# Seven-product projections at the front, and prompt attention A and B two heads at a time in halves of TensorE's array

## The chip, the core and the metric

The kernel runs on one core of a Trainium2 chip. The metric is the device time of one execution in microseconds (us). A core has TensorE (PE; its weight loads are PEld), VectorE (DVE), ScalarE (ACT), GpSimd (POOL) and SyncE (SP, which issues most DMAs), and 16 DMA engines.

## What is computed

One layer of a streaming encoder, on 1024 prompt frames and 8 x 16 sample frames (1152 rows, nine tiles of 128), width 1024:

```python
def project(xn, w_in, b_f, g_qa, g_ka, g_qb, g_kb, g_qm):
    z = xn @ w_in
    qa, ka, va, qb, kb, vb, fl, qm, gates = jnp.split(z, IN_SPLITS, axis=-1)
    qa = rmsnorm(qa.reshape(b, t, H_A, DH_A), g_qa)
...
def gated_merge(o_a, o_b, o_m, gates, w_pa, w_pb, w_pm, w_o):
    g_a, g_b, g_m = jnp.split(jax.nn.sigmoid(gates), N_BRANCH, axis=-1)
    h = g_a * (o_a @ w_pa) + g_b * (o_b @ w_pb) + g_m * (o_m @ w_pm)
    return h @ w_o
...
    xp = xp + gated_merge(o_a, o_b, o_m, gates, w_pa[l], w_pb[l], w_pm[l], w_o[l])
    xp = xp + sq_relu_mlp(xp, g_ffn[l], w_up[l], w_down[l])
```

ka, qb, kb and qm are normalised like qa, and sq_relu_mlp is the square of relu(rmsnorm(x) w_up), times w_down. o_a is attention in a band of nine 64-frame chunks (8 heads of 64, a learned bias by distance), o_b causal attention with summed forget gates added to the scores (8 heads of 64), o_m cross attention into 256 memory tokens (4 heads of 128). Each is computed for the prompt and for the samples, which also read caches. Q and K are normalised per head. K, V, the forget gates and the memory's K and V are outputs too. Everything is float32.

## The kernel before

Most products are made of three matmuls in a fast float32 format (F32R): each operand is split into a high part (ACT copies it to F32R) and a low part (DVE or POOL subtracts), and hi·hi, hi·lo and lo·hi are added in PSUM (`hilo` line 270, `mm3` line 322). Plain float32 matmuls are used for transposes and in the sample attentions.

**Stages.** First the front: x is scaled and split (`x_part`), then `group` (line 387) multiplies, for each of nine row tiles, eight depth tiles of x with a 512-wide block of w_in: V_A, Q_A, K_A, the memory's K and V, and V_B with the eight forget-gate columns (two halves of 260). `head_norm` (line 353) does squares, sums, a power on POOL and two multiplications; `to_T` transposes Q and K and stores them in DRAM.

Then prompt A, sample A, prompt B, sample B, memory for the prompt and the samples: six attentions one after another (`attend`, line 1560). Their engines' orders are written ahead by a planner (`class Plan`, line 50). It runs the attention's tasks against a small cost table, hands each piece to TensorE when its inputs should be ready, and where none is ready takes a *filler* (`fill`, line 133): single depth steps of other products. Fillers are, in this order, `project` (line 624: Q_B, K_B and Q_M, each in two halves 256 wide, with their norms and transposes), `gates` (line 586: 24 feature tiles times three columns of 384 frames, tanh, stored in DRAM) and `merge` (line 723: the products with w_pa, w_pb, w_pm and the gated sum). The order so made is kept on TensorE, DVE, ACT, POOL and SP.

After the last filler come the output projection with w_o and the MLP, which is already done by seven products in place of eight (`Pair`, `DOWN`).

**Prompt A and B** (`prompt_ab`, line 840) run 64 steps: 8 heads times 8 query blocks of 128. For one step: `scores` (line 914) multiplies the block's queries with up to 640 (A) or 1024 (B) keys, in pieces of at most 512, `soften` adds the bias and takes the maximum on DVE, `exp_norm` does the exponential on ACT and the division on POOL or DVE, `transposes` (line 964) turns the probabilities by blocks of 128, `values` (line 1007) multiplies two query blocks at once with V. A head has only 64 dimensions, so the kernel fills the 128 rows twice: Q's high part stands in rows 0 to 63 and its low part in rows 64 to 127 (`qs`), K stands in both halves (`kh`, `kl`), and two matmuls of all rows make the product:

```python
pe.matmul(ps[:, :m], qa, kh[:, ks], start=True, stop=False)
pe.matmul(ps[:, :m], qa, kl[:, ks], start=False, stop=True)
```

V stands likewise in the columns (`vs`: 64 of high part, 64 of low part); the turned probabilities are split into `pth` (ACT) and `ptl` (DVE) on their way out of PSUM, two matmuls a key block, and ACT and DVE add the two halves of the result. PSUM's eight banks are divided z 2 (fillers), tp 3 (transposes), s 2 (scores), pv 1 (values).

The sample attentions place four small float32 matmuls beside each other, in quarters of the array's columns (`tile_position=(0, 32 * pr)`).

Of the kernel before, what the change touches and what calls it, by code (L numbers as in the profile page):

```python
# [49 lines left out]
class Plan:  # L50
# [50 lines left out]
    def bank(self, k):  # L101
        r = self.rel[k]
        return r[len(r) - self.bufs[k]] if len(r) >= self.bufs[k] else 0.0
# [82 lines left out]
def tile_encoder(ctx: ExitStack, tc: tile.TileContext, i, o):  # L186
    nc = tc.nc
    plan = Plan()

    class Engine:  # L190
# [4 lines left out]
        def __getattr__(self, name):  # L195
            f = getattr(self.e, name)

            def call(*a, **k):
                ins = f(*a, **k)  # L199
                if plan.on:  # L200
                    tc.keep_in_program_order(ins)
                return ins
            return call

    class pe:
        @staticmethod
        def matmul(out, lhsT, rhs, **k):
            n = math.prod(rhs.shape[1:])
            plan.now += n * ((2 if "tile_position" in k else 4) if rhs.dtype == F32 else 2 if n < 256 else 1) / 2400 + 0.003
            ins = nc.tensor.matmul(out, lhsT, rhs, **k)  # L210
            if plan.on:
                tc.keep_in_program_order(ins)

        @staticmethod
        def transpose(*a):
            plan.now += math.prod(a[0].shape[1:]) * 2 / 2400
            ins = nc.tensor.transpose(*a)
            if plan.on:
                tc.keep_in_program_order(ins)
# [31 lines left out]
    def banks(**n):  # L251
        with ExitStack() as st:
# [7 lines left out]
    gains = tl(cst, (P, 512), tag="gains")  # L260
    g_of = {"qa": gains[:, 0:64], "qb": gains[:, 64:128], "ka": gains[:, 128:192], "kb": gains[:, 192:256],
            "qm": gains[:, 256:384], "km": gains[:, 384:512]}
# [70 lines left out]
    rm = tl(cst, (P, 2), tag="rm")  # L333
    prj = ExitStack()

    pgs = ExitStack()
    pg = pgs.enter_context(tc.tile_pool(reuse_waits="tile", name="pg", bufs=2, side="right"))
    rb = tl(pg, (P, NT), tag="rb", bufs=1)
    pxs = ExitStack()
    px = pxs.enter_context(tc.tile_pool(reuse_waits="tile", name="px", bufs=2, side="right"))  # L340
    pj = prj.enter_context(tc.tile_pool(reuse_waits="tile", name="pj", bufs=2))
    wp = prj.enter_context(weights(3, 14, "wp"))
    prj.enter_context(banks(z=4, tp=3))
# [4 lines left out]
    for _ in range(18):  # L348
        pe.matmul(ps[:, 0, :], idle, idle, start=True, stop=True)
# [3 lines left out]
    def head_norm(z, sc, gain, dh):  # L353

        nh = HB // dh
        zc = tl(pj, (P, HB), tag="zc")
        act.activation(zc, z, AF.Copy, scale=sc)
        sq = tl(pj, (P, HB), tag="sq", bufs=1)
        act.activation(sq, zc, AF.Square)
        ss = tl(pj, (P, 8), tag="hss")  # L360
        vec.tensor_reduce(ss[:, :nh], sq.rearrange("p (h d) -> p h d", h=nh), AX.X, ALU.add)
        r = tl(pj, (P, 8), tag="hr")
        rstd(ss[:, :nh], r[:, :nh], dh)
        zn = tl(pj, (P, HB), tag="zn", bufs=5)
        v3 = lambda t: t.rearrange("p (h d) -> p h d", h=nh)
        vec.tensor_tensor(v3(zn), v3(zc), r[:, :nh, None].to_broadcast((P, nh, dh)), ALU.mult)
        gps.tensor_tensor(v3(zn), v3(zn), gain[:, None, :].to_broadcast((P, nh, dh)), ALU.mult)
        return zn

    def to_T(zn, dst, t):  # L370
# [4 lines left out]
        act.activation(zt, ps, AF.Copy)  # L375
        act.dma_start(dst.rearrange("(k p) t -> p k t", p=P)[:, :, t * P:(t + 1) * P], zt)


    later = []

    def flush(keep=0):
        while len(later) > keep:
            f = later.pop(0)
            if f:
                f()

    def group(ws, n, handle, pair=None, tiles=TT):
        nb = 2 if n > 512 else 1
        m = n // nb
        for t in range(tiles):  # L390
            zs = []
            for b in range(nb):
                ps = tl(psum["z"], (P, 512), tag="z")
                lhs = cols(xp, t) if pair is None else (lambda k: tuple(s[:, k, t * P:(t + 1) * P] for s in pair))
                mm3(ps[:, :m], lhs, lambda k: tuple(w[:, b * m:(b + 1) * m] for w in ws[k]), KD)
                zs.append(ps[:, :m])
            flush(2)
            later.append(handle(t, *zs))

    def w_rows(src, col, n):  # L400
        return [weight(wp, src[k * P:(k + 1) * P, col:col + n], n) for k in range(KD)]

    def q_tile(b, dh):
        def handle(t, z):
            zn = head_norm(z, rs[:, t:t + 1], g_of["q" + b], dh)
            return lambda: to_T(zn, qT[b], t)
        return handle

    def k_tile(b):
        def handle(t, z):  # L410
            zn = head_norm(z, rs[:, t:t + 1], g_of["k" + b], 64)
            sp.dma_start(o["k" + b][t * P:(t + 1) * P, :], zn)
            return lambda: to_T(zn, kT[b], t)
        return handle

    def v_a(t, z):
        zn = tl(pj, (P, HB), tag="zv")
        act.activation(zn, z, AF.Copy, scale=rs[:, t:t + 1])
        act.dma_start(o["va"][t * P:(t + 1) * P, :], zn)

    def v_b(t, z0, z1):
        zn = tl(pj, (P, HB), tag="zv")
        act.activation(zn[:, 0:260], z0, AF.Copy, scale=rs[:, t:t + 1])
        act.activation(zn[:, 260:512], z1[:, 0:252], AF.Copy, scale=rs[:, t:t + 1])
        act.dma_start(o["vb"][t * P:(t + 1) * P, :], zn)
        vec.scalar_tensor_tensor(lf[:, t, :], z1[:, 252:260], rs[:, t:t + 1], bf, ALU.mult, ALU.add)

    def mem_k(t, z):
        zn = head_norm(z, rm[:, t:t + 1], g_of["km"], 128)
        sp.dma_start(o["mk"][t * P:(t + 1) * P, :], zn)  # L430
        return lambda: to_T(zn, mkT, t)

    def mem_v(t, z):
        zn = tl(pj, (P, HB), tag="zv")
        act.activation(zn, z, AF.Copy, scale=rm[:, t:t + 1])
        act.dma_start(o["mv"][t * P:(t + 1) * P, :], zn)
# [60 lines left out]
    def x_part(c, kh, ks=range(4)):  # L497
        xr = tl(px, (P, 4, CH), tag="xr")
        ks = list(ks)
        k0, k1 = ks[0], ks[-1] + 1  # L500
        src = i["xT"].rearrange("(k p) t -> p k t", p=P)
        sp.dma_start(xr[:, k0:k1, :], src[:, kh * 4 + k0:kh * 4 + k1, c * CH:(c + 1) * CH])
        for k in ks:
            hilo_scaled(xr[:, k, :], xp[0][c][kh][:, k, :], xp[1][c][kh * 4 + k], gcol[:, 0, kh * 4 + k:kh * 4 + k + 1])

    def x_rows(ts):
        for t in ts:
            xt = tl(px, (P, D), tag="xt")
            sp.dma_start(xt, i["x"][t * P:(t + 1) * P, :])
            sum_sq(px, xt, ss[:, t:t + 1])  # L510
            rstd(ss[:, t:t + 1], rs[:, t:t + 1], D)

    ws = []
    ss = tl(cst, (P, TT + 2), tag="ss")
    for k in range(KD):
        x_part(0, k // 4, (k % 4,))
        ws.append(weight(wp, i["w_in"][k * P:(k + 1) * P, V_A:V_A + HB], e=vec if k < 2 else gps))
    x_rows(range(2))
    for kh in range(2):
        x_part(1, kh)  # L520
    x_rows(range(2, 5))
    for kh in range(2):
        x_part(2, kh)
    sp.dma_start(ident, i["ident"])
    sp.dma_start(gains, i["gains"].to_broadcast((P, 512)))

    vec.tensor_scalar_mul(gains[:, 0:128], gains[:, 0:128], 64.0 ** -0.5)
    vec.tensor_scalar_mul(gains[:, 256:384], gains[:, 256:384], 128.0 ** -0.5)
    x_rows(range(5, TT))
    group(ws, HB, v_a)  # L530
    for t in range(2):
        xt = tl(px, (P, D), tag="xt")
        sp.dma_start(xt, i["mem"][t * P:(t + 1) * P, :])
        sum_sq(px, xt, ss[:, TT + t:TT + t + 1])
        rstd(ss[:, TT + t:TT + t + 1], rm[:, t:t + 1], D)
    group(w_rows(i["w_in"], Q_A, HB), HB, q_tile("a", 64))
    sp.dma_start(tri, i["tri"])
    sp.dma_start(bf, i["b_f"].to_broadcast((P, 8)))

    ps = tl(psum["tp"], (P, 4, P), tag="tp")  # L540
    pe.transpose(ps[0:TT, 0, :], rs, ident)
    rt = tl(pj, (TT, P), tag="rt", bufs=1)
    act.activation(rt, ps[0:TT, 0, :], AF.Copy)
    act.dma_start(rsd.rearrange("o (t p) -> (o t) p", p=P), rt)
    pxs.close()
    with tc.tile_pool(reuse_waits="tile", name="mp", bufs=1, side="right") as mp:
        mn = tuple(tl(mp, (P, 8, NMEM), F32R, tag=f"mn{s}") for s in "hl")
        mr = tl(mp, (P, 8, NMEM), tag="mr")
        sp.dma_start(mr, i["memT"].rearrange("(k p) t -> p k t", p=P))
        for k in range(KD):  # L550
            hilo_scaled(mr[:, k, :], mn[0][:, k, :], mn[1][:, k, :], gcol[:, 1, k:k + 1])
# [1472 lines left out]
```

## Time and profile before

| what | value |
|---|---|
| time, three runs | 2044.78, 2052.18, 2049.38 us; median 2049.38 |
| the profiled execution | 2052.52 us; span from the first to the last instruction 2050.7 us |
| TensorE busy | 1994.0 us (97%), 12946 matmul records |
| DVE, ACT, POOL busy | 59%, 47%, 28% |
| DMA | 325.54 MB, 159 GB/s mean |
| TensorE clock granted | 0.994 on average |

How to read it: a group's row names line, engine, operation, output<-input (buffer numbers left out), shape, count, then busy us and mean ns of one, then the idle time before it and what ended that. Matmuls are pipelined, so their single durations overlap; what one costs is read from starts or from a stretch's count. A float32 matmul stands as two records. All operations that the small wrapper classes record have the wrapper's line (L199, L210, L217), so rows are told apart by tile names: z filler or projection, s scores, tp transposes, pv values, wlo and whi the parts of weights.

### The profile page before, as it was taken

The page shows a single profiled execution, that of the slowest core. Times are in us where ns is not written, and L with a number is a line of the kernel's source. Part 1 is how long each engine was busy: PE and PEld are TensorE (multiplying, and loading weights), DVE is VectorE, ACT ScalarE, POOL GpSimd, SP SyncE. Part 2 cuts the span into 40 slices and gives each one's busy share as a digit, 9 for nine tenths or more (in the row PEclk, how much of TensorE's full clock was granted, in tenths as well). Part 3 has the DMA queues.
Part 4 walks back from the last instruction along what each step waited for, and adds up shares of the span by engine and source line. Part 5 has one row for each costly group of instructions (what it writes and reads, how often), then busy time and mean ns, then how long its engine had stood idle before and what let it go on. Part 6 is the DMA issues. An engine that isn't in the chain of part 4 may idle for free. (4 is left out here: it accounts for less than half of the span.)

```text
span 2050.7 us, 35667 instructions
## 1 busy us (share of the span) xinstructions
PE 1994.0 (97%) x12946; PEld 1817.3 (89%) x12946; DVE 1214.4 (59%) x2383; ACT 965.6 (47%) x1950; POOL 568.4 (28%) x650
## 2 busy tenths in 40 slices
PE   9999999999899998899999999989999999999999
PEld 7778999999599997698989997889999998888887
DVE  3444178886269882254254662696555655785775
ACT  6443268886357772254242122564444454453332
POOL 2435066664134551110021010235344431000000
PEclk9999999999999999999999999999999999999999
DMA  8453155554964437745375443225343449663463
GB/s 287 137 176 122 62 136 135 148 131 125 296 179 125 123 92 238 246 131 199 132 246 179 130 144 118 67 92 178 131 144 130 140 157 318 196 200 110 127 194 127
DMA packets 227374, 325.54 MB, mean 159 GB/s; under 512 B 48101, under 2 KB 120950, under 8 KB 227198
## 3 DMA queue, kind: packets, MB, share of 16 engines
q1 hardware_dynamic: 176888, 281.85, 43.9%
q10 hardware_dynamic: 50310, 41.42, 6.5%
q8 instruction: 102, 1.67, 0.4%
q14 instruction: 74, 0.61, 0.1%
HBM read 238.00 MB, written 85.18 MB: 158 GB/s over the span
## 5 line engine op out<-in xcount | busy, mean ns | idle before, releaser
L1625 PE MATMUL b<-r 128*128 128x512 f32 (+2 forms) x2200 | 457.5, 357 | 5.3 <-ACT r L199 3.0
L1625 PEld LDWEIGHTS b<-r 128*128 128x128 f32 x2200 | 379.7, 190 | 63.5 <-ACT r L199 3.9
L199 ACT ACTIVATE r<-fa 128x512 fp32r<-128x512 f32 (+4 forms) x264 | 212.1, 813 | 330.4 <-PE b L1625 281.2
L199 DVE TENSOR_TENSOR r<-fa,r 128x512 fp32r<-128x512 f32 (+4 forms) x264 | 271.5, 1039 | 138.9 <-ACT r L199 133.9
L210 PE MATMUL z<-hi,whi 128*128 128x384 f32 x960 | 300.4, 345 | 10.9 <-ACT whi L199 9.5
L1625 PE MATMUL b<-r,r 128*128 128x320 f32 (+1 forms) x1928 | 288.3, 299 | 4.8 <-DVE r L199 4.7
L1625 PEld LDWEIGHTS b<-r,r 128*128 128x128 f32 x1928 | 271.2, 190 | 6.6 <-DVE r L199 6.6
L210 PE MATMUL z<-hi,wlo 128*128 128x384 f32 x768 | 259.5, 338 | 0.5
L210 PE MATMUL z<-whi,hi 128*128 128x256 f32 (+2 forms) x792 | 255.7, 324 | 1.8 <-DVE lf L199 0.8
L210 PE MATMUL z<-wlo,hi 128*128 128x256 f32 (+2 forms) x792 | 248.6, 314 | 1.9 <-DVE wlo L199 0.9
L210 PE MATMUL z<-whi,lo 128*128 128x256 f32 (+2 forms) x792 | 247.4, 313 | 0.0
L199 POOL TENSOR_TENSOR fa<-fa 128x512 f32<-128x512 f32 x114 | 167.7, 1478 | 246.6 <-ACT fa L199 126.3
L210 PEld LDWEIGHTS z<-hi,whi 128*128 128x128 f32 x960 | 178.5, 189 | 20.7 <-ACT whi L199 12.1
L210 PE MATMUL z<-lo,whi 128*128 128x384 f32 x576 | 194.0, 337 | 0.0
L199 ACT ACTIVATE whi<-wst 128x512 fp32r<-128x512 f32 (+1 forms) x160 | 99.5, 629 | 195.3 <-DMA wst<-in_w_g 72.4
L210 PEld LDWEIGHTS z<-wlo,hi 128*128 128x128 f32 x792 | 150.2, 190 | 14.1 <-DVE wlo L199 3.2
L210 PEld LDWEIGHTS z<-whi,hi 128*128 128x128 f32 x792 | 149.8, 189 | 12.9 <-ACT whi L199 2.5
L210 PEld LDWEIGHTS z<-whi,lo 128*128 128x128 f32 x792 | 149.8, 189 | 9.4 <-DVE lo L199 0.4
L199 DVE TENSOR_TENSOR wlo<-wst,whi 128x512 fp32r<-128x512 f32 (+1 forms) x127 | 96.4, 771 | 102.8 <-ACT whi L199 102.1
L210 PEld LDWEIGHTS z<-hi,wlo 128*128 128x128 f32 x768 | 144.9, 189 | 2.6 <-DVE wlo L199 2.6
L199 ACT ACTIVATE s<-s,nm 128x256 f32<-128x256 f32 (+8 forms) x180 | 122.3, 681 | 41.3 <-DVE nm L199 38.3
L199 POOL TENSOR_SCALAR s<-s,ri 128x640 f32<-128x640 f32 (+8 forms) x100 | 78.1, 783 | 183.9 <-DVE ri L199 148.3
(190 smaller groups left out, 3401.8 us busy)
## 6 DMA issues: line engine op xcount, KB each, us to landing
td<-fa SPq DMA_DIRECT2D x112, 256.0 KB
fa<-td SPq DMA_DIRECT2D x80, 256.0 KB
fa<-in_w_down SPq DMA_DIRECT2D x76, 256.0 KB
fa<-in_w_up SPq DMA_DIRECT2D x32, 512.0 KB
tg<-tg ACTq DMA_DIRECT2D x72, 192.0 KB
th<-tg SPq DMA_DIRECT2D x72, 192.0 KB
wst<-in_w_in SPq DMA_DIRECT2D x48, 256.0 KB
wst<-in_w_g SPq DMA_DIRECT2D x48, 256.0 KB
```

The costliest lines, as they stand in the source:

```text
L199: ins = f(*a, **k)
L210: ins = nc.tensor.matmul(out, lhsT, rhs, **k)
L1625: pin(nc.tensor.matmul(ps, lh, rh, **k))
```

## The change

1. **Projections.** All of w_in's blocks but the gates are now multiplied in the front; `project` is gone from the fillers. Six blocks are taken in three pairs (Q_A, K_A), (V_B, Q_B), (K_B, Q_M). The 1024 prompt rows are taken as even and odd tiles, x's depth as two halves, and a pair's two blocks as left and right: a 2 x 2 by 2 x 2 product, done by seven products of half the depth instead of eight (`products`). The sums of x are made once (`sums`: S1, S2, S4, and S3 in place of the odd tiles' first half), the sums of weights on DVE as they are needed (`makers_of`), from blocks of w_in that are read more than once. Results are summed on DVE from PSUM. The ninth tile (samples) is multiplied the ordinary way beside them. V_A goes the ordinary way in halves of 260 with the forget-gate columns. Q's gain moves into the copy after the transpose. The order of TensorE and DVE from here on is as written.
2. **Prompt A and B** take two heads a step (32 steps): Q and K of two heads lie in rows 0 to 63 and 64 to 127 as they are, each split into high and low, and each head's three matmuls use its half of the rows (`tile_position=(64 * e, 0)`), into a PSUM bank of its own.
3. **Values** are plain float32: the turned probabilities are copied once (ACT or DVE, whichever the planner sees free), and the two heads' matmuls use halves of the columns (`tile_position=(0, 64 * e)`).
4. PSUM in the attentions: z 2, tp 2, s 3, pv 1. The forget gates' sums run during prompt A.

The diff, cut to its core:

```diff
+    prj.enter_context(banks(z=7, tp=1))
...
+    def run(u0, tiles, ks=range(4), free=True):
+        for x, (lhs, key, first, last, then) in enumerate(tiles):
+            put_lo()
...
+                pe.matmul(ps, h, wh, start=first and k == ks[0], stop=False, skip_group_check=True)
+                pe.matmul(ps, h, wl, start=False, stop=False, skip_group_check=True)
+                pe.matmul(ps, l, wh, start=False, stop=last and k == ks[-1], skip_group_check=True)
+                if free and x == len(tiles) - 1:
+                    release(u0 + k)
...
+    def products(u0, left, right, hook=None):
+        even, odd_, last = (lambda t: cols(xp, 2 * t)), (lambda t: cols(xp, 2 * t + 1)), cols(xp, TT - 1)
+        upper = lambda f: lambda k: f(k + 4)
+        of = lambda S, t: lambda k: (S[:, t, 0, k], S[:, t, 1, k])
...
+        run(u0, [(even(t), t, True, True, copy(u3[t])) for t in ts] + [(last, "s", True, False, None)])
+        run(u0 + 4, [(upper(last), "s", False, True, beside(left))]
+            + [(upper(even(t)), "y", True, True, m2(t)) for t in ts])
+        run(u0 + 8, [(of(S2, t), t, False, True, copy(u2[t])) for t in ts])
+        run(u0 + 12, [(odd_(t), t, False, True, copy(u3[t])) for t in ts])
+        run(u0 + 16, [(of(S1, t), "y", True, True, both(t)) for t in ts])
+        for t in ts:
...
+            run(u0 + 20, [(of(S4, t), "y", True, True, plus(u2[t], lambda: right(2 * t, u2[t])))], free=False)
+            run(u0 + 24, [(last, "s", t == 0, False, None)], (t,))
+        run(u0 + 20, [(upper(last), "s", False, True, beside(right))])
...
+        run(u0 + 28, [(upper(odd_(t)), t, False, True, copy(u2[t], lambda t=t: left(2 * t + 1, u2[t]))) for t in ts])
...
+    products(8, q_out("a", 64), k_out("a"))
+    products(40, v_out(o["vb"], rs), q_out("b", 64))
+    products(72, k_out("b"), q_out("m", 128), at_last)
...
             def piece(x, m):
...
-                    pe.matmul(ps[:, :m], qa, kh[:, ks], start=True, stop=False)
-                    pe.matmul(ps[:, :m], qa, kl[:, ks], start=False, stop=True)
-                    plan.spawn(soften(ps, bk, x, m, x + m == nkey))
...
+                    for j, (q, k) in enumerate(((qh, kh), (qh, kl), (ql, kh))):
+                        for e in range(2):
+                            r = slice(64 * e, 64 * e + 64)
+                            pe.matmul(ps[e][1][:, :m], q[r, qc], k[r, ks], start=j == 0, stop=j == 2, tile_position=(64 * e, 0))
...
-            def turn(t, bk, m, dst, last):
-                act.activation(dst[0], t[:, 0:m, :], AF.Copy)
-                yield plan.op("act", m * P)
-                vec.tensor_tensor(dst[1], t[:, 0:m, :], f32(dst[0]), ALU.subtract)
+            def turn(t, bk, m, dst, e, last):
+                k = plan.first(m * P, ("act", 0), ("vec", 0.2))
+                if k == "act":
+                    act.activation(dst, t[:, 0:m, :], AF.Copy)
+                else:
+                    vec.tensor_copy(dst, t[:, 0:m, :])
...
-                    for w in units[h, g][u]:
-                        pe.matmul(pv[:, a * P:e * P], vs[:, kb, :], w[:, r, a * P:e * P],
-                                  start=m == 0, stop=m == 2 * len(plan_) - 1)
+                    for e in range(2):
+                        pe.matmul(pv[64 * e:64 * e + 64, a * P:z * P], vd[:, kb, 64 * e:64 * e + 64],
+                                  units[p, g][e][u][:, r, a * P:z * P], start=m == 0, stop=m == len(plan_) - 1, tile_position=(0, 64 * e))
...
-    plan.bufs = dict(z=2, tp=3, s=2, pv=1)
+    plan.bufs = dict(z=2, tp=2, s=3, pv=1)
...
     def fillers():
-        r = next(g)
-        while r is not None:
-            yield r
-            r = next(g)
...
         yield from gg
         yield from gm
```

In the names of the new order, wa are the split weights, rw the read blocks of w_in, fe the front's buffers (x, later the summed results), sa and sb the sums of x.

More of the change, by code (lines that the diff above doesn't have):

```diff
@@ new lines, in x_rows, with odd, into_odd @@
+    def x_rows(*ts):
+        for t in ts:
+            row_sums(i["x"][t * P:(t + 1) * P, :], ss[:, t:t + 1], rs[:, t:t + 1], row[0])
+            row[0] = 1 - row[0]
+    row = [1]
+    def odd(t):
+        c, j = divmod(2 * t + 1, 3)
+        r = slice(j * P, (j + 1) * P)
+        return xp[0][c][0][:, :, r], [xp[1][c][k][:, r] for k in range(4)]
+    def into_odd(t, src):
+        h, l = odd(t)
+        act.activation(h, src, AF.Copy)
+        for k in range(4):
+            vec.tensor_tensor(l[k], src[:, k, :], f32(h[:, k, :]), ALU.subtract)
@@ new lines, in tile_encoder, with prepare, put_lo, produce @@
+    wt, makers = [], []
+    sources, los = [], []
+    def prepare(u):
+        if len(sources) <= u < len(makers):
+            sources.append(makers[u]())
+    def put_lo():
+        while los:
+            los.pop(0)()
+    def produce(place, lo_now=None):
+        u = len(wt)
+        prepare(u)
+        put_lo()
+        if u == len(makers):
+            return
+        src, then = sources[u]
+        h, l = (x[:, :src.shape[1]] for x in place)
+        act.activation(h, src, AF.Copy)
+        wt.append(place)
+        def lo():
+            (lo_now or vec).tensor_tensor(l, src, f32(h), ALU.subtract)
+            if then:
+                then()
+        los.append(lo)
+        if lo_now:
+            put_lo()
+        else:
+            prepare(u + 1)
@@ new lines, in release, with ask, take, back @@
+    def release(u):
+        if u != NW:
+            produce(wt[u])
+    queue, asked, taken, used = [], [0], [0], set()
+    def ask():
+        while asked[0] < len(queue) and (asked[0] < NR - 4 or asked[0] - (NR - 4) in used):
+            sp.dma_start(raw[4 + asked[0] % (NR - 4)][:, :HB], queue[asked[0]])
+            asked[0] += 1
+    def take():
+        n = taken[0]
+        taken[0] += 1
+        assert n < asked[0]
+        def back():
+            used.add(n)
+            ask()
+        return raw[4 + n % (NR - 4)][:, :HB], back
@@ L371, in to_T, with scale @@
+        def scale():
+            zn = tl(pj, (P, HB), tag="zn") if fresh else z
+            vec.tensor_tensor(v3(zn), v3(z), r[:, :nh, None].to_broadcast((P, nh, dh)), ALU.mult)
+            if gain is not None:
+                vec.tensor_tensor(v3(zn), v3(zn), gain[:, None, :].to_broadcast((P, nh, dh)), ALU.mult)
+            then(zn)
+        in_(1, sums)
+    def to_T(zn, dst, t, g=None):
         ps = tl(psum["tp"], (P, 4, P), tag="tp")
@@ L374, in to_T @@
         zt = tl(pj, (P, 4, P), tag="zt")
-        act.activation(zt, ps, AF.Copy)
+        act.activation(zt, ps, AF.Copy, **({} if g is None else {"scale": g}))
         act.dma_start(dst.rearrange("(k p) t -> p k t", p=P)[:, :, t * P:(t + 1) * P], zt)
[L379 to L398, printed above, removed]
@@ new lines, in k_out, with then, v_out, handle @@
+    def k_out(b):
+        def then(t, zn):
+            sp.dma_start(o["k" + b][t * P:(t + 1) * P, :], zn)
+            in_(2, lambda: to_T(zn, kT[b], t))
+        return lambda t, z: norm(z, rs[:, t:t + 1], 64, lambda zn: then(t, zn), g_of["k" + b])
+    def v_out(dst, scale, fresh=False):
+        def handle(t, *of):
+            zn = of[0] if of[0].shape[1] == HB and not fresh else tl(pj, (P, HB), tag="zn")
+            x = 0
+            for z in of:
+                act.activation(zn[:, x:x + z.shape[1]], z, AF.Copy, scale=scale[:, t:t + 1])
+                x += z.shape[1]
+            act.dma_start(dst[t * P:(t + 1) * P, :], zn)
+        return handle
@@ new lines, in v_a_source, with source @@
+    def v_a_source(k):
+        def source():
+            src = i["w_in"][k * P:(k + 1) * P]
+            sp.dma_start(raw[k][:, :HB], src[:, V_A:V_A + HB])
+            sp.dma_start(raw[k][:, HB:], src[:, V_B + HB:V_B + HB + 8])
+            return raw[k], None
+        return source
+    makers.extend(v_a_source(k) for k in range(KD))
+    for k in range(KD):
+        x_load(0, slice(k, k + 1))
+        produce((slots + more)[k], vec if k < 2 else gps)
+        x_split(0, (k,))
+    x_rows(0)
@@ new lines, in tile_encoder @@
+    sp.dma_start(bf, i["b_f"].to_broadcast((P, 8)))
+    x_load(4)
+    x_split(4)
+    x_load(1, slice(0, 4))
+    x_load(1, slice(4, 8))
+    x_rows(1)
+    x_split(1)
+    x_rows(TT - 1)
+    PAIRS = ((Q_A, K_A), (V_B, Q_B), (K_B, Q_M))
+    for n, pair in enumerate(PAIRS):
+        makers_of(pair, PAIRS[n + 1] if n < 2 else None)
+    queue.extend(i["w_mkv"][k * P:(k + 1) * P, x:x + HB] for x in (0, HB) for k in range(KD))
+    makers.extend([take] * 16)
+    for k in range(4):
+        sp.dma_start(kept[k], rows_(Q_A)(k))
@@ L438, in forget_gates @@
+    mem_products(104, mem_k)
+    fes.close()
+    sbs.close()
+    pgs = ExitStack()
+    pg = pgs.enter_context(tc.tile_pool(reuse_waits="tile", name="pg", bufs=2, side="right"))
+    rb = tl(pg, (P, NT), tag="rb", bufs=1)
+    sp.dma_start(rb, rsd.to_broadcast((P, NT)))
     def forget_gates(pool):
@@ L513, in tile_encoder @@
[L513 to L527, printed above, removed]
@@ L540, in tile_encoder @@
[L540 to L551, printed above, removed]
-        group(w_rows(i["w_mkv"], 0, HB), HB, mem_k, mn, 2)
-        group(w_rows(i["w_mkv"], HB, HB), HB, mem_v, mn, 2)
@@ new lines, in biases @@
+        def biases():
+            for h in range(8):
+                yield from plan.ring(("bias", b), NB)
+                bias = tl(pool, (P, WK), tag="bias", bufs=NB)
+                if b == "a":
+                    sp.dma_start(bias, i["rel"][h])
+                else:
+                    sp.dma_start(bias, ncp[h:h + 1, :].to_broadcast((P, NP)))
+                yield plan.load(400)
+                if b == "a":
+                    gps.memset(bias[0:64, 576:640], NEG)
+                    gps.memset(bias[64:128, 0:64], NEG)
+                    yield plan.op("gps1", 100)
+                else:
+                    yield mask(bias, 7)
+                yield from plan.until(lambda: h // 2 in heads)
+                heads[h // 2][5][h % 2] = bias
+                bias_at[h] = plan.t
@@ L1566, in rest @@
         plan.run([], rest=True)
-    attend("aa", lambda p: prompt_ab("a", p))
+    with tc.tile_pool(reuse_waits="tile", name="fg", bufs=1, side="right") as pool:
+        plan.spawn(forget_gates(pool))
+        attend("aa", lambda p: prompt_ab("a", p))
     attend("sa", lambda p: sample_ab("a", p))
     late["a"] = 0
-    plan.spawn(plan.until(lambda: "projected" in late))
-    plan.run([])
     attend("ab", lambda p: prompt_ab("b", p))
```

670 lines of the change are left out of this document (356 added, 314 removed).

## The prediction

> **What bounds the kernel now.** I read the head of the page first: the busy share of each engine.
>
> ```profile
> span 2050.7 us, 35667 instructions
> ...
> PE 1994.0 (97%) x12946; PEld 1817.3 (89%) x12946; DVE 1214.4 (59%) x2383; ACT 965.6 (47%) x1950; POOL 568.4 (28%) x650
> ```
>
> TensorE (PE) is busy 97% of the span, no other engine over 59%. Next the busy time by stage; I cut at the first matmul of each attention and of the output projection. The rows are, in order: the front, prompt A, sample A, prompt B, sample B, memory prompt, memory sample with the rest of gates and merge, and then output projection and MLP. Columns: start:end, length, busy time (instructions) of PE, PEld, DVE, ACT, POOL, then granted clock, DMA share, GB/s.
>
> ```profile
> 0.00:293.40 293.40, 288.15 (x1659) 248.93 (x1660) 114.91 (x198) 131.73 (x248) 105.44 (x125) 1.00 0.49 153
> 293.40:507.70 214.30, 212.79 (x1768) 210.63 (x1770) 177.56 (x549) 167.20 (x441) 129.74 (x186) 1.00 0.50 133
> 507.70:588.00 80.30, 69.71 (x712) 54.27 (x711) 23.82 (x77) 23.95 (x60) 9.21 (x18) 0.98 0.81 255
> 588.00:791.30 203.30, 203.11 (x1376) 197.86 (x1376) 165.74 (x462) 143.90 (x333) 95.85 (x132) 1.00 0.46 129
> 791.30:889.80 98.50, 83.15 (x752) 65.82 (x752) 26.22 (x79) 26.36 (x63) 8.42 (x22) 0.95 0.77 243
> 889.80:960.90 71.10, 71.10 (x451) 68.16 (x452) 44.57 (x81) 42.14 (x115) 10.19 (x8) 1.00 0.39 133
> 960.90:1213.10 252.20, 243.95 (x1517) 233.68 (x1517) 128.47 (x232) 70.39 (x138) 29.62 (x27) 0.99 0.55 175
> 1213.10:2050.70 837.60, 822.06 (x4729) 737.99 (x4728) 533.11 (x707) 359.90 (x556) 179.93 (x132) 0.99 0.47 153
> ```
>
> In both prompt stages TensorE waits 1.7 us of 417.6: fillers close every hole, so work taken off DVE or ACT there is worth nothing, and work taken off TensorE counts in full, since a filler not used there is used later (the last fillers, the merge, end in the stage of 252.2 us). The last row (837.6 us) is untouched. So the sum goes by TensorE time, plus new waits. Its prices come from stretches of one shape, again busy time in windows: 256 and 260 columns wide; 384; 512.
>
> ```profile
> 200.00:250.00 50.00, 49.18 (x412) 48.98 (x411) 2.90 (x11) 9.88 (x20) 1.28 (x1) 1.00 0.22 72
> 1150.00:1200.00 50.00, 49.54 (x283) 48.67 (x282) 36.33 (x64) 12.62 (x23) 6.82 (x5) 1.00 0.42 125
> 1800.00:1900.00 100.00, 100.00 (x443) 82.84 (x442) 69.90 (x94) 44.64 (x61) 0.00 (x0) 1.00 0.50 152
> ```
>
> Divided: 0.1194 us for 256, 0.175 for 384, 0.2257 for 512, weight load included. (The mean durations of the groups are longer, since matmuls overlap.)
>
> **Part 1, the projections.** Groups of TensorE by shape; each row stands for three of the same count (hi·hi, hi·lo, lo·hi):
>
> ```profile
> L210 PE MATMUL z<-whi,hi 128*128 128x256 f32 x432 | 128.9, 298 | 0.8 <-DVE lf L199 0.8
> L210 PE MATMUL z<-whi,hi 128*128 128x512 f32 x216 | 85.8, 401 | 0.9 <-ACT whi L199 0.7
> L210 PE MATMUL z<-whi,hi 128*128 128x260 f32 x144 | 41.0, 285 | 0.0
> ```
>
> Before: 1296 x 0.1194 + 648 x 0.2257 + 432 x 0.1194 = 352.6 us. After: V_A alone with the gate columns, 432 of 260 (51.6). Each of three pairs has 28 products of four row tiles with half the depth, and four for the ninth tile: 32 x 4 x 3 = 384 matmuls of 512, 1152 in all (260.0). Sum 311.6, **-41.0 us**: 32 from 7/8, 9 from whole 512-wide products. The memory projections stay.
>
> What this costs is DVE in the front. Its prices, by shape:
>
> ```profile
> L199 DVE TENSOR_TENSOR wlo<-wst,whi 128x512 fp32r<-128x512 f32 x119 | 88.1, 748 | 100.9 <-ACT whi L199 100.1 <-issue 0.2
> L199 DVE TENSOR_TENSOR zn<-zc,hr 128x512 f32<-128x512 f32 x20 | 13.9, 693 | 39.4 <-POOL hr L199 39.4
> L199 DVE TENSOR_REDUCE hss<-sq 128x8 f32<-128x512 f32 x18 | 12.3, 682 | 19.0 <-ACT sq L199 19.0
> ```
>
> A pair needs 32 low parts, 16 weight sums and 16 sums of results: 64 x 0.69 = 44 us; nine Q tiles of two operations (12) and nine K tiles of three (19): 75 us against 384 x 0.2257 = 87 us of TensorE. On average DVE keeps up. Locally it does not: from the first S1 product of Q_A/K_A to that pair's end, 168 matmuls (37.9 us), the new order has 53 such operations, 36.6 us at 0.69 and 39.6 at 0.748. A nearby case of a full DVE is this window of prompt A:
>
> ```profile
> 350.00:400.00 50.00, 49.89 (x416) 49.37 (x415) 43.84 (x135) 40.94 (x109) 31.25 (x46) 1.00 0.55 144
> ```
>
> With DVE at 88% TensorE still waited only 0.1 us, but fillers helped there and the front has none. Behind a late DVE stand the results' sums that free a bank (four banks hold running sums, one the ninth tile, two rotate), and TensorE. I take **+10 us** for two such stretches (pairs one and three), between 0 and 25. The extra weight reads (32 blocks of 256 KB a pair for 16) ride on a front whose DMA share is 0.49: nothing; without that cover each block would show, 1.7 us at that row's 153 GB/s. With Q_B, K_B and Q_M their norms and stores move from under prompt A to the front too, past what ACT and POOL (131.73 and 105.44 of 293.4 us busy) do there: room enough, so nothing.
>
> **Part 2, scores.** Counts of one of two equal groups:
>
> ```profile
> L210 PE MATMUL s<-kh,qs 128*128 128x384 f32 x80 | 30.6, 383 | 0.0
> L210 PE MATMUL s<-kh,qs 128*128 128x256 f32 x56 | 17.4, 311 | 0.0
> L210 PE MATMUL s<-kh,qs 128*128 128x512 f32 x40 | 17.2, 429 | 0.8 <-POOL qs L199 0.8
> L210 PE MATMUL s<-kh,qs 128*128 128x128 f32 x16 | 4.4, 275 | 0.0
> ```
>
> Before: 2 x (80 x 0.175 + 56 x 0.1194 + 40 x 0.2257 + 16 x 0.1194) = 63.3 us (128 wide at the price of 256, as the trace has no pure stretch of it). After: three products a head for two, 94.9 us one after another, 47.4 us if the two halves of the rows run side by side. The trace has no product in row halves. The nearest are quarters of the columns, in sample A (timeline of TensorE; start, length, what):
>
> ```profile
> 531.09 0.33 PE L210 MATMUL z<-lo,whi 128*128 128x384 f32 x1
> 531.26 0.34 PE L210 MATMUL z<-hi,wlo 128*128 128x384 f32 x1
> 531.53 1.10 PE L210 MATMUL s<-kd,qb 128*32 128x264 f32 x16
> 532.56 0.44 PE L210 MATMUL z<-hi,whi 128*128 128x384 f32 x1
> 532.84 0.34 PE L210 MATMUL z<-lo,whi 128*128 128x384 f32 x1
> ...
> 537.31 1.08 PE L210 MATMUL pv<-vd,spt 128*32 128x128 f32 x32
> 538.21 0.40 PE L210 MATMUL pv<-v,t 128*32 128x128 f32 x8
> ```
>
> A float32 product is two records; 32 records are eight rounds of four tiles in 0.90 us, 0.1125 us a round. Four tiles do run at once, and the weight loads between rounds are hidden. So I take side by side: **-15.8 us**, the other end +31.6. In the Trainium skill, TensorE: Matmul & The Clock Gate, section The mechanism, a weight load overlaps a running matmul only when its row group differs. By that every round above would show a load and none does: trace and rule differ for columns, and no row shows it for row halves. It is a rival below.
>
> **Part 3, values.**
>
> ```profile
> L210 PE MATMUL pv<-pth,vs 128*128 128x256 f32 x224 | 56.1, 285 | 0.0
> L210 PE MATMUL pv<-pth,vs 128*128 128x128 f32 x80 | 17.7, 231 | 0.0
> ```
>
> Before, with the low parts: 608 x 0.1194 = 72.6 us. After: 112 pairs 256 wide and 40 pairs 128 wide, float32, four and two rounds: (448 + 80) x 0.1125 = 59.4, **-13.2 us**.
>
> **Part 4, in and out of the divided array.** The rows at 531 also price it. Into it, 0.27 us from the last 384 for 0.175: 0.095. Sixteen records 264 wide are 4 x 264/128 x 0.1125 = 0.93 us of 1.03: 0.10. The next 384 takes 0.28: 0.105. Together 0.30 us each time. Before, prompt A and B never leave the whole array. Now, TensorE in prompt A, first before, then after (s: scores, z: filler, tp: transposes):
>
> ```order
> L210 MATMUL s_3429<-kh_2928,qs_2930 128x384
> L210 MATMUL s_3429<-kl_2929,qs_2930 128x384
> L210 MATMUL z_3413<-whi_2561,hi_164_232 128x256
> L210 MATMUL z_3413<-wlo_2562,hi_164_232 128x256
> L210 MATMUL z_3413<-whi_2561,lo_167_235 128x256
> ```
>
> And after, at the same block of 384 keys:
>
> ```order
> L222 MATMUL tp_4100<-ident_203,s_4029 128x128
> L215 MATMUL s_4105<-kh_3835,qh_3837 128x384
> L215 MATMUL s_4107<-kh_3835,qh_3837 128x384
> L215 MATMUL s_4105<-kl_3836,qh_3837 128x384
> L215 MATMUL s_4107<-kl_3836,qh_3837 128x384
> L215 MATMUL s_4105<-kh_3835,ql_3838 128x384
> L215 MATMUL s_4107<-kh_3835,ql_3838 128x384
> L215 MATMUL z_4049<-hi_154_222,whi_3957 128x384
> ```
>
> A block that was two matmuls of one head is six now: two heads (s_4105, s_4107) alternate, with whole-array work on both sides. The whole order has 96 such blocks of scores and 32 of values, in 119 stretches: 119 x 0.30 = **+36 us**, between 0.10 (only one side paid) and 0.35 a time: 12 to 42. Here is the DVE stretch of part 1, before (K_A: low parts were made ahead) and after:
>
> ```order
> L199 TENSOR_REDUCE hss_1705<-sq_1703 128x8
> L199 TENSOR_TENSOR zn_1710<-zc_1701,hr_1707 128x512
> L199 TENSOR_REDUCE hss_1751<-sq_1749 128x8
> L199 TENSOR_TENSOR zn_1756<-zc_1747,hr_1753 128x512
> L199 TENSOR_REDUCE hss_1797<-sq_1795 128x8
> ```
>
> After, in the S1 product of K_A:
>
> ```order
> L203 TENSOR_REDUCE hss_1616<-sq_1602 128x8
> L203 TENSOR_TENSOR rw_252<-rw_252,fe_268 128x512
> L203 TENSOR_TENSOR wa_256<-rw_252,wa_256 128x512
> L203 TENSOR_TENSOR fe_268<-z_1629,fe_268 128x512
> L203 TENSOR_TENSOR fe_268<-fe_268,hr_1577 128x512
> L203 TENSOR_TENSOR fe_268<-fe_268,gains_248 128x512
> ```
>
> Between two reductions there now stand a weight sum (rw), a low part (wa), a bank's sum (z) and two steps of the norm.
>
> **The sum.** -41.0 - 15.8 - 13.2 + 36 + 10 = -24.0 us. Removed at no gain: the low parts of probabilities on ACT and DVE, hidden behind fillers already. A block of scores now waits for two free banks of three instead of one of two; behind it on TensorE stand transposes and fillers, which the written order puts first where the planner sees no bank: nothing, or, should DVE free them late, part of the 1.7 us that prompt A and B wait today. The shorter warm-up, the bias ring and the whole-row loads of V lie beside other work: nothing. The profiled run took 2052.5 us (span 2050.7), 3.1 above the median 2049.4: span 2026.7, run 2028.5, median 2025.4. About 0.3% (6 us) is what a measurement can tell from no change.
>
> **Rivals.**
> - Row halves run one after another (prompt A and B): +47.4, **2072.8**. From 1.5 times the length of one on (24/47.4), the gain is gone. Against it, quarters of columns run at once; for it, no row shows row halves. 0.11.
> - Weight loads stand open in row mode: two of three steps in 96 blocks, 192 loads of 0.189 us (row below), +36: **2062**. 0.07.
>
> ```profile
> L210 PEld LDWEIGHTS z<-whi,hi 128*128 128x128 f32 x792 | 149.8, 189 | 12.9 <-ACT whi L199 2.5
> ```
>
> The Trainium skill's rule on weight loads (same page and section) is this rival.
> - DVE is the bound of the front: waits of 25 to 35 us instead of 10, **2040 to 2050**; and the seven products then save next to nothing. For it, 97% to 104% load in the stretch above; against it, 86% on average. 0.17 (0.04 faster, 0.12 same, 0.01 slower).
> - Going in and out costs 0.10 us: -24, **2001**. 0.10.
>
> The forecast has 0.55, its own range 2011 to 2042 (the bounds of parts 1 and 4). Faster 0.55 + 0.10 + 0.04 = 0.69; same 0.12; slower 0.11 + 0.07 + 0.01 = 0.19. The range leaves out the first two rivals and little more: 2000 to 2056.
>
> **What would show it.** Right: the front longer and prompt A shorter, by the projections that moved; prompt B within some 10 us of 203.3 (less work, dearer ways in and out); the two matmuls of a score pair starting together; a 384 beside a divided stretch 0.1 us late; DVE over 75% in the front. Wrong: the two matmuls of a pair a full length apart; TensorE waiting on DVE for over 25 us in the front; or prompt A and B waiting by more than a few us, which would mean that fillers no longer close the holes.

## The result, and the profile after

The changed kernel took 2035.92 us (median of five runs, 2035.45 to 2041.56) beside 2051.67 for the kernel before; the ratio is 0.9931, 95% interval 0.991 to 0.9951: 14 us faster, where 24 were forecast. The profiled execution took 2041.38 us, 5.5 above the kernel's median. So the sizes of whole changes are taken below from ratios (0.001 is 2.05 us); the traces serve for where the time goes and for the price of single steps.

Head of the page, after:

```profile
span 2039.5 us, 33972 instructions
...
PE 1977.0 (97%) x12338; PEld 1715.7 (84%) x12338; DVE 1232.0 (60%) x2333; ACT 944.8 (46%) x1823; POOL 515.8 (25%) x578
```

Busy time by stage, after, cut and ordered as in the prediction:

```profile
0.00:408.70 408.70, 392.50 (x1990) 330.52 (x1990) 280.93 (x499) 225.58 (x411) 150.17 (x180) 0.99 0.58 176
408.70:585.80 177.10, 177.10 (x1280) 143.20 (x1281) 100.55 (x351) 101.15 (x257) 49.89 (x69) 1.00 0.33 104
585.80:665.60 79.80, 65.21 (x680) 51.10 (x679) 22.50 (x73) 24.20 (x58) 9.53 (x19) 0.94 0.83 278
665.60:877.60 212.00, 212.00 (x1477) 172.54 (x1476) 113.46 (x347) 113.72 (x264) 79.06 (x122) 1.00 0.31 99
877.60:974.00 96.40, 84.69 (x767) 68.47 (x767) 25.32 (x78) 27.65 (x64) 9.80 (x24) 0.93 0.77 244
974.00:1045.60 71.60, 71.60 (x451) 68.83 (x449) 51.07 (x92) 45.88 (x123) 15.51 (x13) 1.00 0.59 194
1045.60:1199.70 154.10, 150.28 (x983) 142.18 (x983) 100.74 (x186) 46.05 (x91) 21.55 (x20) 0.98 0.63 204
1199.70:2039.50 839.80, 823.58 (x4730) 738.86 (x4728) 537.44 (x707) 360.60 (x556) 180.33 (x132) 0.99 0.47 152
```

The front is 115 us longer, prompt A 37 shorter, prompt B 9 longer, the stage that ends the fillers 98 shorter; the output projection begins at 1199.7 instead of 1213.1. In prompt A and B TensorE waits for nothing at all. Its idle time (length less busy time) stands in the front, 16.2 us for 5.3, in sample A and B, 14.6 and 11.7 for 10.6 and 15.4, and in the last filler stage, 3.8 for 8.3. DVE fell from 177.6 to 100.6 us in prompt A.

A block of scores in prompt A, timeline of TensorE (start, length, what, how many):

```profile
503.26 0.33 PE L215 MATMUL z<-hi,wlo 128*128 128x384 f32 x1
503.52 0.39 PE L215 MATMUL s<-kh,qh 64*128 64x256 f32 x2
503.74 0.28 PE L215 MATMUL s<-kl,qh 64*128 64x256 f32 x2
503.86 0.28 PE L215 MATMUL s<-kh,ql 64*128 64x256 f32 x2
504.07 0.45 PE L215 MATMUL z<-hi,whi 128*128 128x384 f32 x1
504.35 0.33 PE L215 MATMUL z<-lo,whi 128*128 128x384 f32 x1
```

The two heads' matmuls start together (each row is two), and the second pair is followed by the third after 0.12 us, the price of one matmul of 256: the two run side by side, and that step shows no weight load. Around them stands the cost of the divided array: the first pair starts 0.26 us after a 384 instead of 0.175, the second pair 0.22 after the first instead of 0.12, the next whole matmul 0.21 after the third pair, and that one then takes 0.28.

The front in 25 us windows, and what TensorE waited for there (waits by what released them: us in total, times, longest):

```profile
25.00:50.00 25.00, 22.56 (x167) 22.36 (x167) 20.14 (x50) 18.71 (x47) 4.65 (x8) 0.88 0.84 288
...
325.00:350.00 25.00, 25.00 (x124) 20.53 (x124) 23.99 (x43) 17.10 (x29) 15.24 (x21) 1.00 0.64 194
...
375.00:400.00 25.00, 17.33 (x80) 14.50 (x79) 14.44 (x40) 6.34 (x11) 4.83 (x11) 0.93 0.42 144
```

```profile
PE z L215 <- ACT hi L203: 5.0, 2, 2.5
PE z L215 <- DVE wa L203: 3.8, 3, 2.7
```

At 325 DVE is busy 24.0 of 25 us and TensorE does not wait. It waits at the two ends: for the split of x in the first 50 us and where the front hands over to the gates (375 to 400). In the middle DVE's low parts are late by 1.1 us in all, at 154 us.

### The profile page after: what moved, and what is told of

Same layout as the page of the kernel before. It is cut to its first block, busy times and chain, and to the rows that moved or that the text cites. A ratio compares the mean times of both kernels' runs of the same rounds, so it can differ in the third digit from the quotient of the medians.

```text
span 2039.5 us, 33972 instructions
## 1 busy us (share of the span) xinstructions
PE 1977.0 (97%) x12338; PEld 1715.7 (84%) x12338; DVE 1232.0 (60%) x2333; ACT 944.8 (46%) x1823; POOL 515.8 (25%) x578
## 5 line engine op out<-in xcount | busy, mean ns | idle before, releaser
L215 PE MATMUL z<-hi,whi 128*128 128x384 f32 x960 | 318.1, 363 | 11.6 <-ACT whi L203 8.3
L215 PE MATMUL z<-wa,hi 128*128 128x512 f32 (+1 forms) x732 | 203.1, 365 | 6.8 <-ACT hi L203 5.0
L215 PEld LDWEIGHTS z<-wa,hi 128*128 128x128 f32 x732 | 128.8, 192 | 26.9 <-ACT hi L203 5.4
L203 POOL TENSOR_SCALAR s<-s,ri 128x256 f32<-128x256 f32 (+8 forms) x106 | 79.3, 752 | 268.5 <-DVE ri L203 222.7
L215 PE MATMUL z<-wa,lo 128*128 128x512 f32 (+1 forms) x366 | 130.4, 359 | 0.0
L203 DVE CUSTOM_DVE_ANT_0 s<-s,bias 128x384 f32<-128x384 f32 (+4 forms) x144 | 71.0, 526 | 90.0 <-PE s L215 86.6
L215 PEld LDWEIGHTS z<-lo,whi 128*128 128x128 f32 x576 | 110.0, 191 | 0.1
L222 PE MATMUL tp<-ident,s 128*128 128x128 f32 (+1 forms) x680 | 101.9, 277 | 7.7 <-POOL s L203 6.8
L203 DVE TENSOR_TENSOR fa<-b,fa 128x256 f32<-128x256 f32 (+1 forms) x160 | 71.0, 450 | 54.8 <-PE b L1849 43.7
L203 ACT ACTIVATE whi<-wst 128x512 fp32r<-128x512 f32 x88 | 55.1, 629 | 104.6 <-DMA wst<-in_w_g 40.6
```

## The experiments

**What each part is worth.** The front of after with before's attentions (`prompt_ab` and the banks z 2, tp 3, s 2, pv 1 put back):

> The changed front with the prompt attentions A and B of the kernel before (one head a step, products on the whole array). Theory: by the trace of after, the halves save 29 us of matmuls and cost about 50 us in ways in and out of the divided array, so they lose about 21 us: 2036 - 21 = 2015. By the forecast's own price (36 us of ways) they lose 7: 2029. Rival, that the front's VectorE work eats the gain of the projections and the halves bring it: 2041 to 2052, and TensorE waiting on VectorE for over 25 us in the front.

Measured 2041.14 us, ratio 0.9966 (0.9955 to 0.9978). My first theory, that the halves lose 21 us, fell: beside after's 0.9931 they gain 7. Next, eight ordinary products in the front instead of seven (the core of the diff):

```diff
-        run(u0, [(even(t), t, True, True, copy(u3[t])) for t in ts] + [(last, "s", True, False, None)])
...
+        for u, out in ((u0, left), (u0 + KD, right)):
+            for t in range(TT):
+                run(u, [(cols(xp, t), "y", True, True, copy(t, out))], range(KD), free=t == TT - 1)
```

> All projections in the front, 512 wide, but by ordinary products: eight half-depth products where after has seven, no sums of x, of weights or of results. Theory: VectorE's sums lie beside TensorE and the seventh-eighths save 3 x 48 x 0.2257 = 32.5 us, so this takes 2036 + 32 = 2068. By the forecast's sum (10 us of VectorE waits come with the seven): 2058. Rival, VectorE bounds the front and the seven products save next to nothing: 2036 to 2043.

> The kernel with eight ordinary products again, with another order of the eight buffers that take the results (in the first one the ninth tile's buffer was taken again before its norm was done, so its K rows came out as other numbers). All theories: as the first, 2056, that is 20 us over after: 32.5 of matmuls less some 10 us of pauses that the seven products bring at the start and the end of the front.

Measured 2055.8 us, 1.0038 (1.0024 to 1.0052), and 2057.91 us, 1.0041 (1.0025 to 1.0057). The first wrote over one tile's results too early; the second does not, and stands in the table below. At last neither part, only the move into the front (the last kernel with before's `prompt_ab`):

> Neither the seven products nor the halves: all projections in the front, 512 wide, by eight ordinary products, and the prompt attentions of the kernel before. By the forecast's terms: 432 x 3 matmuls of 256 become 216 x 3 of 512, 9 us less, 2041. Theory: taken out of the fillers, the projections are missed later, where TensorE waits or runs at a lower clock after waits (12 us by the trace of the front alone): 2054 to 2062, slower than before.

Measured 2063.5 us, 1.0073 (1.0049 to 1.0097). The four make a square:

| ratio to before | before's attentions | halves |
|---|---|---|
| all projections in front, ordinary | 1.0073 | 1.0041 |
| all projections in front, seven products | 0.9966 | 0.9931 |

Seven products bring 22 us on either side, the halves 7 on either side (each 5 to 6 us either way, by the intervals), and moving the projections out of the fillers loses 15, where 512-wide products should have won 9. In the kernel with the move alone, the front, sample A, sample B and the last filler stage:

```profile
0.00:433.10 433.10, 422.50 (x2138) 357.17 (x2139) 156.09 (x283) 184.51 (x344) 138.81 (x177) 0.99 0.43 135
...
640.80:715.10 74.30, 61.23 (x653) 44.96 (x652) 21.71 (x71) 22.60 (x55) 7.86 (x16) 0.98 0.81 265
...
922.00:1019.50 97.50, 76.46 (x720) 58.92 (x720) 28.10 (x83) 30.01 (x70) 12.08 (x25) 0.93 0.80 254
...
1095.40:1227.50 132.10, 123.16 (x809) 113.05 (x809) 89.38 (x165) 41.25 (x83) 21.95 (x20) 0.95 0.63 206
```

TensorE idles 10.6, 13.1, 21.0 and 8.9 us there, 54 in sum, against 39 in the same four of before (5.3, 10.6, 15.4, 8.3): 14 more, of which 5 stand in the front and 8 in the two sample stages. And the clock in the last one is 0.95 for 0.99, so what is left to do takes longer.

It is not that the projections had stood in the waits of the sample stages. In before, the fillers of prompt A are nearly all projections (256 wide), those of sample A are gates (384 wide) already; the first line is prompt A, the second sample A:

```profile
L210 PE MATMUL z<-whi,hi 128*128 128x256 f32 x318 | 95.6, 301 | 0.0
L210 PE MATMUL z<-hi,whi 128*128 128x384 f32 x70 | 25.2, 360 | 0.0
```

The filler matmuls recorded in sample A and B are gates in both kernels, but fewer: 157 and 223 after the move, 211 and 256 before. What TensorE waits for in sample B after the move:

```profile
PE z L215 <- ACT whi L203: 7.3, 2, 5.0
PE tp L222 <- POOL s L203: 4.9, 2, 2.5
PE s L215 <- DMA kd<-in_cbk: 4.7, 3, 3.3
```

Before, the same three were 4.4, 0.5 and 5.0 us. So it is not the waits for the caches' loads that grew, but those for the gates' own weights and for the probabilities from POOL. Why the planner's order came out so was not followed up.

**Where the halves' price went.** Products of zeros, once in the middle of each score block, once ahead of it:

```diff
+                        if j == 1:
+                            pe.matmul(ps[0][1][:, :P], zero, kh[:, k0 * P + x:k0 * P + x + P], start=False, stop=False)
```

> After, with one whole-array product more in each of the 96 blocks of scores (128 wide, of zeros, added to the scores), between the second pair and the third, so that each block goes out of the divided array and in again: 96 ways more. Theory: 96 x (0.12 + 0.40) = +50 us, 2086. By the forecast's 0.30 a way: 96 x 0.42 = +40, 2076. Rival, a way costs 0.10 and the loss lies elsewhere: 96 x 0.22 = +21, 2057.

> The same 96 whole-array products of zeros, but ahead of each block, where the array is undivided anyway: no way more. All theories: 96 x 0.12 = +11.5 us, 2047. The difference to the run with the product inside, divided by 96, is the price of one way in and out: 0.40 by the theory, 0.30 by the forecast, 0.10 by the rival.

Measured 2088.63 us, 1.0193 (1.0174 to 1.0211), and 2053.53 us, 1.0024 (1.0013 to 1.0034). Prompt A and B of the first, then of the second:

```profile
408.10:598.00 189.90, 189.90 (x1277) 144.79 (x1276) 99.14 (x344) 98.60 (x252) 50.21 (x73) 1.00 0.29 92
...
682.00:909.90 227.90, 227.90 (x1494) 177.73 (x1493) 111.71 (x347) 114.59 (x264) 72.58 (x119) 1.00 0.27 88
```

```profile
408.10:580.00 171.90, 171.90 (x1276) 142.25 (x1274) 98.98 (x344) 98.76 (x252) 49.91 (x73) 1.00 0.32 102
...
666.00:875.70 209.70, 209.70 (x1493) 175.80 (x1492) 112.22 (x347) 114.25 (x264) 71.29 (x119) 1.00 0.29 95
```

The same matmuls and the same fillers, 18.0 + 18.2 us apart: 0.38 us a way in and out, for 96 ways. (Why the products ahead cost 19 us by the ratio, and not 11.5, was not followed up; another placing of fillers alone moves 5 to 9 us, as shown below.) Then the blocks with the first head's three products ahead of the second's:

```diff
-                    for j, (q, k) in enumerate(((qh, kh), (qh, kl), (ql, kh))):
-                        for e in range(2):
+                    for e in range(2):
+                        for j, (q, k) in enumerate(((qh, kh), (qh, kl), (ql, kh))):
```

> After, with each block's three score products of the first head issued before the three of the second, instead of in pairs. Theory: pairs run side by side and matmuls in the same rows one after another, so a block takes six lengths, or five where the third of one head and the first of the other overlap, instead of three: 32 to 47 us more, 2068 to 2083. Rival, the two halves run one after another anyway: no change, 2036.

Measured 2039.3 us, 0.9939 (0.9917 to 0.9962): no change. My theory, one matmul after another in the same rows and the second head behind the first, fell, but the rival's reason is wrong too. Its timeline:

```profile
441.89 0.39 PE L215 MATMUL s<-kh,qh 64*128 64x256 f32 x2
442.12 0.29 PE L215 MATMUL s<-kl,qh 64*128 64x256 f32 x2
442.24 0.29 PE L215 MATMUL s<-kh,ql 64*128 64x256 f32 x2
```

Although they are issued in turn, the heads' products still start in pairs: the second head's first one, three places later in the program, runs beside the first head's first (10 ns behind it in the records). The Trainium skill, TensorE: Matmul & The Clock Gate, The mechanism, says that matmuls start and end strictly in program order; this trace differs. The Trainium skill, TensorEngine Tiling (Array Packing), Key Properties, says that tiles execute independently and that a change of the tiling mode drains TensorE; the pairs here and the 0.38 us of a way agree.

So TensorE's own work got dearer, as the sum had it: -29 for the products, and for the ways 87 x 0.38 (scores) + 23 x 0.34 (values) + 9 x 0.58 (a value block with a score block behind it; the last two prices are from starts in the timeline of after) = 46, together +17. A count of the fillers shows it. Filler matmuls alone, prompt A and B, of the front alone and of after:

```profile
408.70:616.20 207.50, 139.26 (x682) 115.69 (x681) 16.00 (x29) 0.00 (x0) 1.00 0.45 130
...
689.10:894.40 205.30, 117.57 (x579) 99.35 (x579) 13.22 (x24) 0.00 (x0) 1.00 0.45 130
```

```profile
408.70:585.80 177.10, 100.34 (x460) 76.29 (x459) 10.51 (x19) 0.00 (x0) 1.00 0.33 104
...
665.60:877.60 212.00, 121.37 (x577) 96.55 (x576) 13.34 (x24) 0.00 (x0) 1.00 0.31 99
```

Less 0.175 us a filler, the attentions' own time is 412.8 - 220.7 = 192.1 us in the first and 389.1 - 181.5 = 207.6 in the second, +15.5. But the two stages are 24 us shorter and leave 224 fillers, 39 us, for later, and later TensorE waits less. Sample B and the last filler stage of the front alone, to be read beside 11.7 and 3.8 us of idle time in after:

```profile
894.40:993.70 99.30, 78.96 (x720) 61.11 (x720) 28.11 (x83) 29.89 (x70) 12.18 (x25) 0.90 0.80 249
...
1069.40:1201.20 131.80, 122.01 (x810) 112.35 (x810) 89.48 (x164) 41.51 (x83) 21.41 (x20) 0.97 0.62 205
```

That is 20.3 and 9.8 us, 14.6 more than after: about what TensorE's own work lost. Is it DVE's lighter work? The low parts put back, unread:

```diff
+                dead = tl(pool, (P, UK * P), mybir.dt.bfloat16, tag="dead", bufs=1)
+                vec.tensor_tensor(dead[:, :m * P].rearrange("p (k c) -> p k c", k=m), t[:, 0:m, :], dst, ALU.subtract)
+                t_ = plan.op("vec", m * P)
```

> After, with one VectorE subtraction more for each copy of turned probabilities in prompt A and B, whose result nobody reads (the low parts that the change removed); TensorE's own work is the same. Theory of the first four runs: a lighter VectorE shortens the attentions, so fewer fillers are used there and more are left for the holes of sample B and the last stages; put back, 8 to 13 us are lost there: 2044 to 2049. Rival, the step of the prediction that called the low parts hidden and worth nothing: 2036, no change.

Measured 2049.06 us, 0.9988 (0.9975 to 1.0002), 12 us over after. Prompt A and B:

```profile
409.20:595.90 186.70, 186.70 (x1330) 152.81 (x1329) 136.46 (x438) 104.38 (x267) 61.59 (x85) 1.00 0.32 102
...
674.00:903.30 229.30, 229.30 (x1572) 189.46 (x1571) 155.78 (x432) 122.66 (x287) 84.46 (x127) 1.00 0.30 97
```

TensorE is 100% busy in both kernels, and DVE's extra 78 us still make the stages 27 us longer, filled with fillers that are used up there. (The added operation also holds the transposes' PSUM bank longer, which this run does not tell apart from DVE's load.) How much of the 12 is chance of where fillers fall?

```diff
-    LAT = 0.45
+    LAT = 0.55
```

> After, with the planner's allowance for the way from one engine to the next at 0.55 us instead of 0.45: the same instructions, the same work, only the fillers fall at other places in the six attentions. It measures how much the placing of fillers alone moves the time. If by 3 us or less, then the 11 us of the run with the low parts put back belong to VectorE's work; if by 6 us or more, that run says little.

Measured 2041.02 us, 0.9958 (0.9941 to 0.9975): 5.5 us, between the bounds I had set. The same at 0.35, in the kernel of `hand3` (below):

> The rearranged end of the front, with the planner's allowance at 0.35 us instead of 0.45. A second measure of what the placing of fillers alone moves (the first, at 0.55, gave 5.5 us more). If placing is chance, this lands within 6 us of 2034 on either side, 2028 to 2040; if fewer fillers left at the end of prompt B mean more waiting from sample B on (1288 recorded ones left: 15 to 18 us of waits; 1083 to 1144: 27 to 30), the waits there follow that count in this run too.

Measured 2043.29 us, 0.9962 (0.9948 to 0.9976), 9 us over `hand3` and outside the 6 us I had allowed. Its sample B and last filler stage:

```profile
843.60:941.90 98.30, 84.64 (x788) 71.16 (x788) 26.62 (x80) 28.10 (x65) 9.67 (x23) 0.95 0.77 245
...
1012.50:1198.40 185.90, 174.94 (x1112) 166.41 (x1112) 108.20 (x200) 53.38 (x106) 30.12 (x27) 0.97 0.63 196
```

It had the most fillers left after prompt B (1432) and yet waited 13.7 + 11.0 us, against 12.7 + 3.8 in `hand3`, so the count left doesn't set the waits: that theory fell. Placing alone moved the time by 5 and 9 us. The halves' 7 us were measured twice but with one plan for each attention, so that they are worth more than nothing is not settled; that DVE's work costs time under a busy TensorE stands on 12 us against that noise and is not shown either.

**The end of the front.** ScalarE in after, then TensorE's wait behind it:

```profile
371.63 0.61 ACT L203 ACTIVATE hi<-rw 128x512 fp32r<-128x512 f32 x1
377.92 0.63 ACT L203 ACTIVATE whi<-wst 128x512 fp32r<-128x512 f32 x1 [5.68 <-DMA wst<-in_w_g]
378.45 0.61 ACT L203 ACTIVATE hi<-rw 128x512 fp32r<-128x512 f32 x1
```

```profile
380.65 2.81 PE L215 MATMUL z<-wa,sa 128*128 128x512 f32 x11 [2.74 <-DVE wa L203]
```

On ScalarE's queue the gates' first split waits for its load ahead of an odd tile's split, whose low parts stand on DVE ahead of the memory's last weights. The splits in the written order:

```diff
+        in_order.append(act)
         into_odd(t, x)
+        in_order.remove(act)
...
+    in_order.append(act)
     begin(next(gg)(0))
```

> After, with ScalarE held to the written order at the end of the front: the split of the gates' first weights, which waits 5.7 us for a load, no longer stands ahead of the split of an odd row tile and of the memory's last weights. Theory: TensorE's waits of 4.7 us before 381 us go, and most of the slow clock that follows the pause: -4 to -6, 2031. Rival, the last weights are late for another reason (their loads, or VectorE): no change, 2036.

Measured 2039.49 us, 0.9947 (0.993 to 0.9963): nothing gained. Those waits were gone, and this one had come:

```profile
392.96 1.11 PE L222 MATMUL tp<-ident,zn 128*128 128x128 f32 x4 [10.59 <-ACT zt L203]
```

So the memory's copies had to come ahead too (the order lifted behind `begin`, and `zn = kept[t] if fresh`):

> After, with the end of the front rearranged once more: ScalarE splits the odd row tiles before the gates' first weights, the copies of the memory's transposed K stand before the second of these, and the memory's V goes out of a free buffer instead of one that waits for the store of K. In the run before this one the wait had only moved: TensorE's 4.7 us before 381 us were gone, but its last transposes waited 10.6 us for a copy behind those splits. Theory: now neither is left, and -3 to -6 us against after: ratio 0.990 to 0.992 to the kernel before. Rival: the gates' first weights land no earlier, the wait moves again and nothing changes: 0.993 to 0.995.

Measured 2033.84 us, 0.9916 (0.9897 to 0.9936), the lowest of all; against after 3 us, within the intervals. The window in place of after's 17.33 of 25 us:

```profile
375.00:400.00 25.00, 20.49 (x99) 17.83 (x98) 16.29 (x42) 8.16 (x15) 4.78 (x11) 0.93 0.51 158
```

## Why the prediction came out as it did

Direction and range held; the size was 14 for 24 us. Two parts were wrong in opposite directions, and that they nearly cancelled is luck: the front alone gained 7 us where the sum has 31 (-41 and +10), and the halves gained 7 where the sum has a loss of 7.

- **Projections, -41 and +10.** The 32 us of seven eighths came, less pauses: 22 by the square, 20 and 24 by the length of the front (408.7 us for 428.3 in `eight_b`, and for 433.1 in the move alone). TensorE's idle time there is 7 us more with seven products than with eight (16.2 for 9.0, 17.9 for 10.6), near the 10 that I took. But the pauses are not those that I meant: DVE's low parts were late by 1.1 us in the middle, and with DVE at 24.0 of 25 us TensorE did not wait; the rest stands at the front's start and end, where loads and the order on ScalarE's queue decide. The rival of a DVE-bound front is refuted.
- **The step that failed** is "a filler not used there is used later", on which "work taken off TensorE counts in full" rests, and with it the 9 us for 512-wide products. Moving the projections alone lost 15. In that profile TensorE idles 14 us more in four stages, and its mean granted clock is 0.990 for 0.994, some 8 us over the span (an estimate): -9 + 14 + 8 = +13. The waits that grew are shown above; why they grew stays open.
- **Scores -15.8 and values -13.2.** Side by side, as taken; with the ways they give +17 for the attentions' own time, where the fillers' count gave +15.5. Of the two rivals on row halves the first is refuted by the pairs' starts, the second but for a part: the first step of a block shows 0.10 us, not two of three steps 0.189 each.
- **In and out, +36.** Mis-sized: 46 by after's starts, over my upper bound of 42 (and far from the rival of 0.10 a time), since the first step of a block is late too (0.22 us for 0.12) and a change between row and column halves costs extra (0.58). For scores the zeros show 0.38, for 0.30.
- **"Removed at no gain: the low parts"** is in doubt. The halves came to -7 where I had +7, although TensorE itself lost the 15.5 us: it waits 14.6 us less in sample B and the last filler stage. Whether a shorter DVE brought that or only another placing of the fillers, which alone moved these waits from 16.5 to 24.7 us, is not shown.

The narrower range of the prediction, 2011 to 2042, is not the sum of the bounds that it names: those of parts 1 and 4 give 1991 to 2046. Of the signs of being right one did not come: DVE stood over 75% only in parts of the front (280.93 of 408.70 us, 69%). Of the signs of a wrong mechanism none came, and yet one step was wrong: none of them watched the sample stages, where time was lost.

## What to carry to other kernels

A pool of fillers does not pay moved work back in full: here the projections' matmuls should have got 9 us shorter by the move, and the kernel got 15 us longer, with more waiting in the sample stages. So a forecast that counts the bottleneck engine's work alone needs a term for the waits of the stages that draw on the same fillers. Nor can other engines' work be called free because fillers keep TensorE at 100%: a slower stage uses up more of them, though what that costs is not settled here. And where a planner places fillers, measure first what another placing alone moves (here 5 and 9 us) before a smaller gain is believed.

## What the runs showed of the hardware

- The two row halves worked off their matmuls independently of the order between them: issued three and three, they still ran in pairs, started at 441.89, 442.12 and 442.24 us.
- Going into row halves and back cost 0.38 us for a block of scores (36.2 us for 96 ways).
- After the handover's pauses TensorE ran slower for a while. Fillers of 384 in after start 0.32 us apart from 392.7 to 395.9 us, later 0.17; the granted clock from 390 to 395 is 0.76:

```profile
394.27 0.53 PE L215 MATMUL z<-lo,whi 128*128 128x384 f32 x1
394.59 0.53 PE L215 MATMUL z<-hi,wlo 128*128 128x384 f32 x1
...
396.81 0.34 PE L215 MATMUL z<-hi,wlo 128*128 128x384 f32 x1
396.99 0.34 PE L215 MATMUL z<-hi,whi 128*128 128x384 f32 x1
```

The mean granted clock fell from 0.994 to 0.987; taken over the span of 2039.5 us that is some 14 us (an estimate; 8 of them in the move alone, 0.990), a term that the forecast lacked. The Trainium skill, TensorE: Matmul & The Clock Gate, What's actually happening, puts the clock after idle at half; the trace comes near it (0.32 us a step for 0.175).
